# GpSimd's elementwise work outside the gated-MLP stage moved to the vector engine, in a two-layer fp32 trunk

## The chip, the cores and the metric

One of the eight cores of a Trainium2 chip runs the whole program; the other cores are idle. The metric is the device time of one execution in microseconds (us), taken as the median of several executions. The engines of the core are TensorE (PE, matrix products), VectorE (DVE, elementwise work and reductions), ScalarE (ACT, activations and copies), GpSimd (POOL, elementwise work here) and SyncE (SP, which issues most of the DMAs). Each has its own queue of instructions and takes them in order; semaphores tie the queues together.

## The reference

Two layers of a diffusion trunk, in float32. 512 latent tokens and 256 context tokens of width 1024 go through the same weights; the second (last) layer has outputs for the latent tokens alone.

```python
h = modulate(rms_norm(x, mix_pre_g[l]), sh1, sc1)
p = h @ w_in[l]                                   # 1024 x 8704
q = apply_rope(q_heads(p, q_norm_g[l]), cos, sin) # 8 heads of 128
k, v = kv_heads(p[..., K_OFF:GU_OFF], k_norm_g[l])# 2 key/value heads
attn = latent_attention(q, k_all, v_all)          # softmax over context + latent keys
# three branches, merged by sigmoid gates:
a_out = attn @ w_attn_o
g_out = chunk_spatial_gate(gelu(gu), rms_norm(gelu(gv)), ws, bs) @ w_gmlp_o
c_out = conformer_conv(...)                       # 31 taps, layer norm, silu, @ w_conv_o
y = (ga * a_out + gg * g_out + gc * c_out) @ w_out
x = x + g1 * rms_norm(y, mix_post_g[l])
h2 = modulate(rms_norm(x, ffn_pre_g[l]), sh2, sc2)
x = x + g2 * rms_norm(jnp.square(jax.nn.relu(h2 @ w_ff1)) @ w_ff2, ffn_post_g[l])
```

## The kernel before

Every large product is made of three products of rounded parts. `wload` fetches a 512 KB weight tile into `raw` (two buffers, `wraw`, and in some stages a few more, `xraw`), ScalarE rounds it to `hi` (`whi`, L171), and a second engine writes the rest `lo = raw - hi` (`wlo`, L174); there are four buffers each of `whi` and `wlo`. Which engine makes `wlo` is an argument, `pool_lo`: True is GpSimd, False the vector engine. Activations are split the same way by `split` (L178 on ScalarE, L179 on the vector engine). TensorE then runs hi*hi, hi*lo and lo*hi (`gemm_t` L192, `gemm_n` L206, `streamed` L494).

A layer has these stages, one behind the other, each with its own pool of SBUF buffers:

- attention. Keys and values, then four pairs of query heads. One softmax step is 128 queries of one head: scores (L635), row maximum (L639, vector), the negative maximum times the scale (`nb`, L642, vector), the exponential on ScalarE (L645), the reciprocal of its sum (L647, vector), the scaling of `Pm` by it (L648, GpSimd), transposes (L658), the split of the transposed tile (L661 ScalarE, L662 vector) and the product with the values (L669). Transposes come two steps behind the scores. In between TensorE works on fill: the projections of the next pair of heads (`q_stage`), the attention output (`attn_o`) and the sigmoid gates (`gate_a`). `rope` (L565 to L568) rotates queries and keys; its third product (L567) is on GpSimd.
- the gated-MLP stage with the 31-tap convolution on the vector engine (`gmlp_conv`), then the rest of the convolution branch (`conv_out`).
- `w_out` by `natural`, in units of 256 columns. The last unit of a token group is followed by `post_norm` (L440 to L452, the residual) and `pre_norm` (L398, transposes, L424 to L428), whose result the feed-forward part reads.
- the feed-forward part in four chunks `ch`: `up` makes relu (L1174, ScalarE), its square (L1175, GpSimd) and the split; `streamed` or `natural` brings it down to `Y`, which in the last chunk is multiplied by the gain (L1216, GpSimd) before the last norms.

The order of each engine's queue is not the order of the code: a scheduler that walks a simulated timeline lays the instructions out, with its own idea of how long each takes. So an operation that changes its engine also changes its place among its new neighbours, and can move neighbours on other engines.

Of the kernel before, what the change touches and what calls it, by code (L numbers as in the profile page):

```python
# [54 lines left out]
def trunk_kernel(ctx: ExitStack, tc: tile.TileContext, x, c, ctx_in, c_ctx, ada_w, ada_b, mix_pre_g, mix_post_g,  # L55
# [152 lines left out]
    def wload_n(src, pool_lo=False):  # L208
        return [wload(src[0:512], 4, 256, pool_lo), wload(src[512:1024], 4, 256, pool_lo)]
# [291 lines left out]
    def attention(l, hT, T, last, md, w_kv=None):  # L501
# [58 lines left out]
        def rope(o, C, S):  # L560

            ov = o[:, 0:4, :].rearrange("p i (h d) -> p i h d", h=2)
            for h in range(2):
                t2 = t_([P, 4, HD], "rt2", 1)
                nc.vector.tensor_tensor(t2[:, :, 0:64], ov[:, :, h, 64:], S[:, :, 0:64], ALU.mult)  # L565
                nc.vector.tensor_tensor(t2[:, :, 64:], ov[:, :, h, 0:64], S[:, :, 64:], ALU.mult)
                nc.gpsimd.tensor_tensor(ov[:, :, h, :], ov[:, :, h, :], C, ALU.mult)  # L567
                nc.vector.tensor_tensor(ov[:, :, h, :], ov[:, :, h, :], t2, ALU.add)  # L568

        def to_heads(o, h, g, ntok, tag, bufs):  # L570
# [12 lines left out]
            return hi, lo  # L583

        def q_stage(p, q):
            ws = wload_n(W[:, Q0 + 256 * p:Q0 + 256 * p + 256], True)
            o = t_([P, NT, 256], "pn", 1)
            for i0 in range(0, NT, 2):
                ps = ps1()
                for i in range(2):  # L590
                    gemm_n(ps[:, i * 256:(i + 1) * 256], (i0 + i) * P, ws, hT)
                    yield 2.6
                nc.scalar.copy(o[:, i0:i0 + 2, :], ps.rearrange("p (i c) -> p i c", c=256))
            rq = head_rstd(o, NT)
            sc = t_([P, 12], "sc", 2)
            nc.vector.tensor_scalar(sc[:, :2 * NT], rq[:, :2 * NT], SCALE, None, op0=ALU.mult)
            nsc = t_([P, 12], "nsc", 2)
            nc.vector.tensor_scalar(nsc[:, :2 * NT], rq[:, :2 * NT], -SCALE, None, op0=ALU.mult)
            rope(o, Cq, Sq)
            q[p] = (o, sc, nsc, p // 2)  # L600
# [11 lines left out]
        for i in range(6):  # L612
            for h in range(2):
                t = k_nat[:, i, h * HD:(h + 1) * HD]
                nc.gpsimd.tensor_scalar(t, t, rs[:, 2 * i + h:2 * i + h + 1], 1.0, op0=ALU.mult, op1=ALU.mult)
        rope(k_nat, Ck, Sk)
        q = {}
        for _ in q_stage(0, q):
# [6 lines left out]
        def S_step(qT, qs, h, i):  # L625
# [19 lines left out]
            nc.scalar.activation(Pm[:, :nk], ps[:, :nk], AF.Exp, bias=nb, scale=sc[:, col:col + 1], accum_out=sm)  # L645
            rc = t_([P, 1], "rc", 4)
            nc.vector.reciprocal(rc, sm)  # L647
            nc.gpsimd.tensor_scalar(Pm[:, :nk], Pm[:, :nk], rc, 1.0, op0=ALU.mult, op1=ALU.mult)  # L648
            return Pm

        def T_step(Pm, PT, attn, kv, i):
# [23 lines left out]

        def attn_o(p, attn):
            for u in range(2):
                w = wload(w_attn_o[l, p * 256:(p + 1) * 256, u * 512:(u + 1) * 512], 2, 512, True)
                for cc in range(4):
                    cidx = u * 4 + cc  # L680
                    if p == 0:
# [15 lines left out]
                        gated(cidx)  # L697

        def gated(cidx):
            nc.gpsimd.tensor_tensor(acc[cidx], acc[cidx], sga[cidx], ALU.mult)  # L700
            nc.scalar.dma_start(md[cidx], acc[cidx])

        def gate_tile(p, cidx):
# [18 lines left out]

        def gate_a(p, cidx):
            off = GATE0 + cidx * P
            w = wload(W[:, off:off + P], KB, P, True)
            sg = gate_tile(p, cidx)
            for s0, n in parts:
                ps = ps1()
                gemm_t(ps, w, hT, T, parts=[(s0, n, 0)])
                nc.scalar.activation(sg[:, s0:s0 + n], ps[:, :n], AF.Copy if p < 4 else AF.Sigmoid)  # L730
                yield 24 * n / 2400
            if p == 0:
                spilled[cidx] = dram.tile([P, T], F32, name=nm("sgd"))
                nc.sync.dma_start(spilled[cidx], sg)
            else:
                sga[cidx] = sg
# [308 lines left out]
    with stage("start", 6):  # L1045
# [36 lines left out]
                next(small, None)  # L1082
        for _ in small:
            pass
        w_kv = wload_kv(0, True, (0, 1))
        ada = [ada_shift_scale(j) for j in range(4)]
        next(ada[0])
        x_columns(LAT)
        w_kv += wload_kv(0, True, (2, 3))
        x_columns(CTXG)  # L1090
        for j in range(4):
            if j < 3:
# [7 lines left out]
    for l in range(DEPTH):  # L1100
# [25 lines left out]
        with stage("ffn", 4 if last else 2):  # L1126
# [35 lines left out]
            with here(ACT_E):  # L1162
                root = o_([P, 12], "rsq", 2)
                nc.scalar.activation(root[:, 0:1], eps, AF.Sqrt)
            natural(w_out[l], mh, [[g] for g in groups], 1, sink, after, True)
            Y = [t_([P, D], "Y", NT) for _ in range(NT)]
            for ch in range(4):
                fs = [(o_([P, T], "hT", 16, F32R), o_([P, T], "hT", 16, F32R)) for _ in range(8)]

                def up(j, w, s0, n):  # L1170
                    ps = ps2()
                    gemm_t(ps, w, h2, T, parts=None if n == T else [(s0, n, 0)])
                    f = t_([P, T], "ff", 2)
                    nc.scalar.activation(f[:, :n], ps[:, :n], AF.Relu)  # L1174
                    nc.gpsimd.tensor_tensor(f[:, :n], f[:, :n], f[:, :n], ALU.mult)  # L1175
                    hi, lo = fs[j]
                    split(hi[:, s0:s0 + n], lo[:, s0:s0 + n], f[:, :n])

                def w_up(j):
                    col = ch * 1024 + j * P  # L1180
                    return wload(w_ff1[l, :, col:col + P], KB, P, ch == 0)

                rest = range(8)
                if ch == 0:
# [19 lines left out]
                def sink2(grp, u, ps):  # L1204
# [7 lines left out]
                    if ch == 3:  # L1212
                        s = slice(u * 256, (u + 1) * 256)
                        squares(grp, u, lambda i: Y[grp[0] + i][:, s])
                        for i in range(grp[1]):
                            nc.gpsimd.tensor_tensor(Y[grp[0] + i][:, s], Y[grp[0] + i][:, s], gb[grp[2]][:, s], ALU.mult)  # L1216

                def after2(g):
                    post_norm(X, Y, g, ssq[g], out if last else None, last and g[0] == 2)
# [42 lines left out]
```

## Time and profile before

| what | value |
|---|---|
| three executions | 2683.68, 2689.81, 2682.62 us; median 2683.68 |
| the profiled execution | 2690.7 us, of which the span of its instructions is 2688.9 |
| mean granted TensorE clock | 0.989 of full speed |
| TensorE busy | 2608.4 us (97% of the span) |
| vector engine busy | 1552.3 us (58%) |
| ScalarE busy | 1076.1 us (40%) |
| GpSimd busy | 914.7 us (34%) |
| HBM | 111 GB/s over the span |

"Busy" is the sum of the time in which an engine had an instruction in work. A busy TensorE is a matter of records whose ends are modelled, so 97% says that it hardly waited, not that it was at its peak. The granted clock is the share of full speed that TensorE was given, here either 1 (2.4 GHz) or one half (1.2 GHz) in a stretch. Every time below is of the profiled execution.

### The profile page before, as it was taken

Reading aid. Unit: us, or ns where it says so; the run is one execution under the profiler, and the core shown is the slowest. Engines: PE = TensorE matmul, PEld = TensorE weight load, DVE = VectorE, ACT = ScalarE, POOL = GpSimd, SP = SyncE. Lnnn points to the kernel's source line nnn. Section 1 sums busy time; section 2 is a strip of 40 time slices with the busy share of each in tenths; the row PEclk is TensorE's granted clock in tenths of the full one; section 3 lists DMA queues with packets and bytes.
Section 4 is the critical chain, followed back from the end, with each engine's and each line's share of the span. In section 5 each row is a group of like instructions: output and inputs, shape, how many; then the busy total and the mean of one; then the engine's idle time right before and its main releaser. Section 6 shows DMA issues by size and latency. Waiting matters only on the chain.

```text
span 2688.9 us, 37915 instructions
## 1 busy us (share of the span) xinstructions
PE 2608.4 (97%) x15133; PEld 2277.3 (85%) x15133; DVE 1552.3 (58%) x2325; ACT 1076.1 (40%) x1848; POOL 914.7 (34%) x648
## 2 busy tenths in 40 slices
PE   6999999999999998999999999999999999999998
PEld 4989988888888898888888899888888888988888
DVE  4635735578864548445564367665479845633335
ACT  3546533443234635422121255555243234533324
POOL 2423336465463203402010133434555510421113
PEclk8999999999999999999999999999999999999999
DMA  6210134232345344243454342212433455433333
GB/s 233 61 56 32 32 98 138 73 93 85 105 135 173 105 160 141 79 127 112 138 188 133 118 157 72 65 32 67 126 102 102 141 155 176 137 118 100 97 95 110
DMA packets 322241, 300.13 MB, mean 112 GB/s; under 512 B 11517, under 2 KB 268817, under 8 KB 322065
## 3 DMA queue, kind: packets, MB, share of 16 engines
q1 hardware_dynamic: 309360, 271.20, 32.6%
q10 hardware_dynamic: 12704, 26.51, 2.8%
q8 instruction: 119, 1.95, 0.3%
q14 instruction: 58, 0.47, 0.1%
HBM read 275.63 MB, written 22.04 MB: 111 GB/s over the span
## 4 chain that ended last, share of the span: by engine, by line
PE 84%; DVE 9%; ACT 3%; DMA 3%; issue 1%; POOL 1%; SPq 0%; ACTq 0%; DVEq 0%; POOLq 0%
PE ps L192 44%; PE ps L494 16%; PE pq L192 7%; PE ps L206 6%; PE pq L206 3%; PE pq L669 3%; PE ps L635 2%; PE ps L658 1%; DVE wlo L174 1%; ACT whi L171 1%; PE ps L919 1%; DVE hB L428 1%; PE ps L532 1%; DMA xraw<-in_ada_w_dram 1%; DMA wraw<-in_w_in_dram 0%
## 5 line engine op out<-in xcount | busy, mean ns | idle before, releaser
L192 PE MATMUL ps<-hB,whi 128*128 128x512 f32 (+1 forms) x2272 | 595.3, 360 | 3.9 <-ACT hB L427 1.6
L174 POOL TENSOR_TENSOR wlo<-wraw,whi 128x1024 fp32r<-128x1024 f32 x160 | 388.3, 2430 | 519.4 <-ACT whi L171 507.2
L171 ACT CAST whi<-wraw 128x1024 fp32r<-128x1024 f32 x261 | 274.3, 1051 | 649.0 <-PE ps L192 325.3
L192 PEld LDWEIGHTS ps<-hB,whi 128*128 128x128 f32 x2272 | 389.7, 189 | 71.3 <-ACT ff L1174 2.3
L837 DVE SCALAR_TENSOR_TENSOR cy<-G,cw,cy 128x768 f32<-128x768 f32 (+1 forms) x464 | 404.3, 887 | 11.5
L192 PE MATMUL ps<-hB,wlo 128*128 128x512 f32 (+1 forms) x1136 | 373.2, 359 | 0.0
L494 PE MATMUL ps<-whi,hT 128*128 128x512 f32 x1152 | 357.1, 390 | 0.0
L1175 POOL TENSOR_TENSOR ff<-ff 128x512 f32<-128x512 f32 (+2 forms) x76 | 111.9, 1473 | 627.1 <-ACT ff L1174 626.9
L192 PE MATMUL ps<-hT,whi 128*128 128x512 f32 (+1 forms) x1408 | 319.1, 344 | 0.6 <-ACT gu L915 0.6
L494 PEld LDWEIGHTS ps<-whi,hT 128*128 128x128 f32 x1152 | 216.3, 188 | 45.7 <-issue 0.8
L192 PEld LDWEIGHTS ps<-hT,whi 128*128 128x128 f32 x1408 | 221.3, 189 | 34.4 <-ACT gu L915 1.1
L206 PE MATMUL ps<-whi,hT 128*128 128x256 f32 x1280 | 235.5, 286 | 0.7 <-ACT whi L171 0.7
L192 PEld LDWEIGHTS ps<-hB,wlo 128*128 128x128 f32 x1136 | 200.5, 189 | 32.0 <-DVE wlo L174 0.2
L494 PE MATMUL ps<-wlo,hT 128*128 128x512 f32 x576 | 224.1, 389 | 0.0
L174 DVE TENSOR_TENSOR wlo<-wraw,whi 128x1024 fp32r<-128x1024 f32 x101 | 133.8, 1326 | 154.6 <-ACT whi L171 151.2
L171 ACT CAST whi<-xraw 128x1024 fp32r<-128x1024 f32 x109 | 114.3, 1049 | 246.7 <-PE ps L494 116.9
L174 DVE TENSOR_TENSOR wlo<-xraw,whi 128x1024 fp32r<-128x1024 f32 x91 | 113.1, 1244 | 166.0 <-ACT whi L171 165.7
L206 PEld LDWEIGHTS ps<-whi,hT 128*128 128x128 f32 x1280 | 202.1, 194 | 1.4 <-ACT whi L171 0.9
L192 PE MATMUL ps<-hT,wlo 128*128 128x512 f32 x704 | 190.4, 344 | 0.0
L206 PE MATMUL ps<-wlo,hT 128*128 128x256 f32 x640 | 182.2, 285 | 1.3 <-DVE wlo L174 1.3
L343 POOL TENSOR_TENSOR asum<-asum,aprod 128x512 f32<-128x512 f32 x84 | 111.3, 1325 | 108.6 <-ACT aprod L341 66.1
L648 POOL TENSOR_SCALAR Pm<-Pm,rc 128x768 f32<-128x768 f32 (+1 forms) x80 | 68.4, 856 | 215.0 <-DVE rc L647 157.4
(300 smaller groups left out, 4654.2 us busy)
## 6 DMA issues: line engine op xcount, KB each, us to landing
wraw<-in_w_in_dram SPq DMA_DIRECT2D x134, 512.0 KB, 3.7
xraw<-in_w_ff_dram SPq DMA_DIRECT2D x89, 512.0 KB, 4.0
wraw<-in_w_ff_dram SPq DMA_DIRECT2D x63, 512.0 KB, 3.9
xraw<-in_ada_w_dram SPq DMA_DIRECT2D x39, 512.0 KB, 4.7
wraw<-in_ada_w_dram SPq DMA_DIRECT2D x33, 512.0 KB, 3.8
araw<-in_ada_w_dram SPq DMA_DIRECT2D x48, 256.0 KB, 2.9
xraw<-in_w_out_dram SPq DMA_DIRECT2D x18, 512.0 KB, 8.4
wraw<-in_w_attn_o_dram SPq DMA_DIRECT2D x16, 512.0 KB, 3.9
```

The source lines that it names most:

```text
L171: nc.scalar.copy(hi, raw)
L174: e.tensor_tensor(lo, raw, hi.bitcast(F32), ALU.subtract)
L192: nc.tensor.matmul(ps[:, d0:d0 + n], wt[:, k, c0:c0 + P], xt[:, s0:s0 + n], start=k == 0 and j == 0, stop=k == nk - 1 and j == 2)
L206: nc.tensor.matmul(o, xt[:, tok0:tok0 + P], wt, start=k == 0 and j == 0, stop=k == nk - 1 and j == 2)
L343: nc.gpsimd.tensor_tensor(sums[r], sums[r], t, ALU.add)
L428: nc.vector.tensor_tensor(lo[:, s], t, hi[:, s].bitcast(F32), ALU.subtract)
L494: nc.tensor.matmul(o, xt[:, tok], wt[:, k, :], start=kt == k == j == 0, stop=kt == 3 and k == 1 and j == 2)
L635: nc.tensor.matmul(ps[:, s0 - key0:s0 - key0 + n], a[:, i * P:(i + 1) * P], b[:, s0:s0 + n], start=m == 0, stop=m == 2)
L648: nc.gpsimd.tensor_scalar(Pm[:, :nk], Pm[:, :nk], rc, 1.0, op0=ALU.mult, op1=ALU.mult)
L669: nc.tensor.matmul(po[:, :256], a[:, kt0 + kt, vs], b[:, kt, :], start=kt == 0 and m == 0, stop=kt == nkt - 1 and m == 2)
L837: nc.vector.scalar_tensor_tensor(done if t == TAPS - 1 else y, G[:, :, t:t + 256], cw[:, t * 8 + cidx:t * 8 + cidx + 1], y, op0=ALU.mult, ...
L1175: nc.gpsimd.tensor_tensor(f[:, :n], f[:, :n], f[:, :n], ALU.mult)
```

## The change

Outside `gmlp_conv` each elementwise instruction of GpSimd becomes one of the vector engine, with the same operands. Two differ in form: the square of the feed-forward part now multiplies the product in PSUM with the relu, and the scalings have one scalar in place of two. What stays on GpSimd are the gated-MLP stage, the sums `asum` (L343) of the modulation vectors beside it, and two adds at the very end (L450). Clearing of tiles stays there too.

```diff
@@ rope
-                nc.gpsimd.tensor_tensor(ov[:, :, h, :], ov[:, :, h, :], C, ALU.mult)
+                nc.vector.tensor_tensor(ov[:, :, h, :], ov[:, :, h, :], C, ALU.mult)
@@ q_stage
-            ws = wload_n(W[:, Q0 + 256 * p:Q0 + 256 * p + 256], True)
+            ws = wload_n(W[:, Q0 + 256 * p:Q0 + 256 * p + 256])
@@ attention, keys
-                nc.gpsimd.tensor_scalar(t, t, rs[:, 2 * i + h:2 * i + h + 1], 1.0, op0=ALU.mult, op1=ALU.mult)
+                nc.vector.tensor_scalar(t, t, rs[:, 2 * i + h:2 * i + h + 1], None, op0=ALU.mult)
@@ S_step
-            nc.gpsimd.tensor_scalar(Pm[:, :nk], Pm[:, :nk], rc, 1.0, op0=ALU.mult, op1=ALU.mult)
+            nc.vector.tensor_scalar(Pm[:, :nk], Pm[:, :nk], rc, None, op0=ALU.mult)
@@ attn_o
-                w = wload(w_attn_o[l, p * 256:(p + 1) * 256, u * 512:(u + 1) * 512], 2, 512, True)
+                w = wload(w_attn_o[l, p * 256:(p + 1) * 256, u * 512:(u + 1) * 512], 2, 512)
@@ gated
-            nc.gpsimd.tensor_tensor(acc[cidx], acc[cidx], sga[cidx], ALU.mult)
+            nc.vector.tensor_tensor(acc[cidx], acc[cidx], sga[cidx], ALU.mult)
@@ gate_a
-            w = wload(W[:, off:off + P], KB, P, True)
+            w = wload(W[:, off:off + P], KB, P)
@@ the start
-        w_kv = wload_kv(0, True, (0, 1))
+        w_kv = wload_kv(0, False, (0, 1))
-        w_kv += wload_kv(0, True, (2, 3))
+        w_kv += wload_kv(0, False, (2, 3))
@@ w_out and feed-forward
-            natural(w_out[l], mh, [[g] for g in groups], 1, sink, after, True)
+            natural(w_out[l], mh, [[g] for g in groups], 1, sink, after)
-                    nc.gpsimd.tensor_tensor(f[:, :n], f[:, :n], f[:, :n], ALU.mult)
+                    nc.vector.tensor_tensor(f[:, :n], ps[:, :n], f[:, :n], ALU.mult)
-                    return wload(w_ff1[l, :, col:col + P], KB, P, ch == 0)
+                    return wload(w_ff1[l, :, col:col + P], KB, P)
-                            nc.gpsimd.tensor_tensor(Y[grp[0] + i][:, s], Y[grp[0] + i][:, s], gb[grp[2]][:, s], ALU.mult)
+                            nc.vector.tensor_tensor(Y[grp[0] + i][:, s], Y[grp[0] + i][:, s], gb[grp[2]][:, s], ALU.mult)
```

Three places show what the scheduler makes of it on the vector engine. The first is layer 0 behind `w_out`, where the residual of the first 256 tokens (`X_9233`, `X_9234`) is followed by their second norm (`rsv_9673` to `rs_9672`, then L398). Before:

```order
L452 SCALAR_TENSOR_TENSOR X_9233<-Y_9239,rs_9656,X_9233 128x1024
L452 SCALAR_TENSOR_TENSOR X_9234<-Y_9240,rs_9656,X_9234 128x1024
L1154 TENSOR_TENSOR Y_9241<-ps_9749,Gb_9262 128x256
L1154 TENSOR_TENSOR Y_9242<-ps_9749,Gb_9262 128x256
L142 TENSOR_SCALAR rsv_9673<-ss_9669 128x2
L146 RECIPROCAL rst_9677<-rsq_9675 128x2
```

The same place now:

```order
L452 SCALAR_TENSOR_TENSOR X_9233<-Y_9239,rs_9656,X_9233 128x1024
L452 SCALAR_TENSOR_TENSOR X_9234<-Y_9240,rs_9656,X_9234 128x1024
L174 TENSOR_TENSOR wlo_9875<-wraw_9871,whi_9873 128x1024
L1154 TENSOR_TENSOR Y_9241<-ps_9749,Gb_9262 128x256
L1154 TENSOR_TENSOR Y_9242<-ps_9749,Gb_9262 128x256
L174 TENSOR_TENSOR wlo_9881<-wraw_9877,whi_9879 128x1024
L142 TENSOR_SCALAR rsv_9673<-ss_9669 128x2
L146 RECIPROCAL rst_9677<-rsq_9675 128x2
```

Two weight splits that stood in GpSimd's queue (`wlo_9875`, `wlo_9881`) have come between the residual and the norm; five more follow before the second norm of the next 256 tokens.

The second place is a softmax step of layer 1 (row maximum `mx_16164`, its product `nb_16166`), with two products of `rope` for the next heads in between. Before:

```order
L639 TENSOR_REDUCE mx_16164<-ps_16157 128x1
L565 TENSOR_TENSOR rt_2590_16274<-pn_16001,S_14844 128x4x64
L566 TENSOR_TENSOR rt_2590_16274<-pn_16001,S_14844 128x4x64
L642 TENSOR_TENSOR nb_16166<-mx_16164,nsc_15671 128x1
L647 RECIPROCAL rc_16171<-sm_16169 128x1
```

The same place now:

```order
L174 TENSOR_TENSOR wlo_16561<-wraw_16557,whi_16559 128x1024
L639 TENSOR_REDUCE mx_16164<-ps_16157 128x1
L565 TENSOR_TENSOR rt_2590_16274<-pn_16001,S_14844 128x4x64
L566 TENSOR_TENSOR rt_2590_16274<-pn_16001,S_14844 128x4x64
L174 TENSOR_TENSOR wlo_16567<-wraw_16563,whi_16565 128x1024
L642 TENSOR_TENSOR nb_16166<-mx_16164,nsc_15671 128x1
```

One split stands ahead of the row maximum, one between it and `nb`.

The third place is a softmax step of context queries in layer 0 (`mx_1887`, `nb_1889`). Before:

```order
L639 TENSOR_REDUCE mx_1887<-ps_1883 128x1
L642 TENSOR_TENSOR nb_1889<-mx_1887,nsc_1005 128x1
L662 TENSOR_TENSOR PT_1860<-ps_1861,PT_1859 128x6x128
L578 TENSOR_TENSOR qT_1878<-ps_1870,qT_1877 128x512
L647 RECIPROCAL rc_1894<-sm_1892 128x1
```

The same place now:

```order
L174 TENSOR_TENSOR wlo_2463<-wraw_2459,whi_2461 128x1024
L639 TENSOR_REDUCE mx_1887<-ps_1883 128x1
L662 TENSOR_TENSOR PT_1860<-ps_1861,PT_1859 128x6x128
L578 TENSOR_TENSOR qT_1878<-ps_1870,qT_1877 128x512
L642 TENSOR_TENSOR nb_1889<-mx_1887,nsc_1005 128x1
```

A split is ahead of the row maximum, and `nb` has fallen behind two other splits. SP's queue, which issues the weight loads, differs only by neighbours that changed places.

## Rows read from the trace of the kernel before

**Rows 1.** The page's part 1: busy time, share of the span, instructions.

```profile
PE 2608.4 (97%) x15133; PEld 2277.3 (85%) x15133; DVE 1552.3 (58%) x2325; ACT 1076.1 (40%) x1848; POOL 914.7 (34%) x648
```

**Rows 2.** Busy time of each engine by stretch; columns as its first line says.

```profile
core 0: us, PE busy (x) PEld busy (x) DVE busy (x) ACT busy (x) POOL busy (x), PEclk, DMA share, GB/s
0.00:37.40 37.40, 14.67 (x95) 9.69 (x95) 20.68 (x47) 17.89 (x30) 10.62 (x16) 0.88 0.89 305
...
100.00:402.00 302.00, 290.94 (x1992) 267.42 (x1991) 166.44 (x364) 147.21 (x330) 108.56 (x83) 0.99 0.17 56
402.00:1005.00 603.00, 595.91 (x3424) 518.37 (x3424) 385.65 (x428) 235.29 (x313) 280.41 (x202) 0.99 0.38 119
1005.00:1072.00 67.00, 60.19 (x435) 57.09 (x435) 55.03 (x93) 40.01 (x91) 27.84 (x10) 0.92 0.48 143
...
1605.00:1690.00 85.00, 79.84 (x626) 77.67 (x625) 64.42 (x146) 47.02 (x121) 31.22 (x29) 0.96 0.29 89
1690.00:1876.00 186.00, 176.74 (x1143) 157.26 (x1142) 114.74 (x225) 101.77 (x201) 75.62 (x54) 0.99 0.16 51
...
2275.00:2345.00 70.00, 63.12 (x488) 61.32 (x487) 46.74 (x75) 39.74 (x90) 27.89 (x15) 0.95 0.59 190
...
2677.70:2688.90 11.20, 2.82 (x24) 2.62 (x22) 5.29 (x16) 2.84 (x8) 3.91 (x4) 0.79 0.24 94
```

**Rows 3.** GpSimd's groups by line: count, busy us, mean ns, idle before.

```profile
L174 POOL TENSOR_TENSOR wlo<-wraw,whi 128x1024 fp32r<-128x1024 f32 x160 | 388.3, 2430 | 519.4 <-ACT whi L171 507.2 <-PE ps L919 11.8
L1175 POOL TENSOR_TENSOR ff<-ff 128x512 f32<-128x512 f32 (+2 forms) x76 | 111.9, 1473 | 627.1 <-ACT ff L1174 626.9
L648 POOL TENSOR_SCALAR Pm<-Pm,rc 128x768 f32<-128x768 f32 (+1 forms) x80 | 68.4, 856 | 215.0 <-DVE rc L647 157.4 <-PE pq L192 16.2 <-DVE nb L642 14.5
L1216 POOL TENSOR_TENSOR Y<-Y,Gb 128x256 f32<-128x256 f32 x40 | 39.1, 995 | 72.6 <-ACT junk L1145 72.6
```

**Rows 4.** The vector engine's groups, shapes kept apart.

```profile
L174 DVE TENSOR_TENSOR wlo<-wraw,whi 128x1024 fp32r<-128x1024 f32 x101 | 133.8, 1326 | 154.6 <-ACT whi L171 151.2 <-PE ps L970 3.0
...
L690 DVE TENSOR_TENSOR acc<-acc,pq 128x512 f32<-128x512 f32 x48 | 32.8, 684 | 27.8 <-PE pq L192 27.8
...
L1154 DVE TENSOR_TENSOR Y<-ps,Gb 128x256 f32<-128x256 f32 x40 | 15.0, 417 | 10.9 <-ACT junk L1145 10.7
...
L398 DVE TENSOR_SCALAR xn<-X,rs 128x1024 f32<-128x1024 f32 x6 | 4.1, 748 | 0.0
```

**Rows 5.** Timelines of DVE and of POOL around 178 us: start, us, instruction.

```profile
172.35 0.16 DVE L642 TENSOR_TENSOR nb<-mx,nsc 128x1 f32<-128x1 f32 x1
...
178.93 1.80 DVE L642 TENSOR_TENSOR nb<-mx,nsc 128x1 f32<-128x1 f32 x1
...
178.37 2.34 POOL L174 TENSOR_TENSOR wlo<-wraw,whi 128x1024 fp32r<-128x1024 f32 x1 [4.25 <-ACT whi L171]
```

**Rows 6.** From 1000 to 1085 us: the chain's shares by line; DVE's and POOL's timelines.

```profile
by line: PE ps L192 26.1%; PE ps L206 16.2%; DVE X L452 10.9%; DVE hB L428 10.2%; DVE wlo L174 8.7%; PE pq L403 4.3%; DVE rsv L142 4.1%; ACT whi L171 3.5%; DVE Y L1154 3.2%; issue 2.9%; DVE Y L398 2.0%; DVE hf L424 1.9%; ACT junk L1145 1.6%
...
1043.77 5.19 DVE L428 TENSOR_TENSOR hB<-hf,hB 128x256 fp32r<-128x256 f32 x2
...
1039.69 6.43 POOL L174 TENSOR_TENSOR wlo<-xraw,whi 128x1024 fp32r<-128x1024 f32 x2 [12.30 <-ACT whi L171]
```

**Rows 7.** DVE's timeline behind `w_out` of layer 1.

```profile
2302.54 2.48 DVE L452 SCALAR_TENSOR_TENSOR X<-Y,rs,X 128x1024 f32<-128x1024 f32 x2
...
2309.93 2.38 DVE L148 TENSOR_TENSOR rst<-rst 128x2 f32<-128x2 f32 x1
2312.34 2.29 DVE L149 SCALAR_TENSOR_TENSOR rst<-rst,rsv 128x2 f32<-128x2 f32 x1
```

**Rows 8.** DVE's timeline in attention of layer 1.

```profile
1742.60 2.59 DVE L566 TENSOR_TENSOR rt<-pn,S 128x256 f32<-128x256 f32 x1
```

**Rows 9.** DVE's timeline at the start.

```profile
17.09 2.22 DVE L135 SCALAR_TENSOR_TENSOR rst<-rst,rsv 128x2 f32<-128x2 f32 x1
```

**Rows 10.** Busy time in one stretch of attention, columns as in rows 2.

```profile
268.00:335.00 67.00, 66.11 (x460) 60.92 (x458) 51.28 (x113) 34.58 (x75) 23.20 (x21) 1.00 0.10 32
```

## The prediction

> **What bounds the kernel now.** I read the page's busy times first: TensorE is busy 97% of the span, the vector engine 58%, GpSimd 34% [rows 1]. So the change can give back only time in which TensorE waits, or in which its clock is halved after a wait. The view by stretch says where that is [rows 2]: stretch less PE's busy time is 22.7 us at the start (37.4 - 14.7), 11.1 in layer 0's attention (100 to 402), 7.1 in 402 to 1005, 6.8 between `w_out` and the feed-forward part of layer 0 (1005 to 1072), 5.2 between the layers (1605 to 1690), 9.3 in layer 1's attention (1690 to 1876), 6.9 behind `w_out` of layer 1 (2275 to 2345) and 8.4 at the end. The five stretches in which GpSimd's moved work lies hold 39 us of waits (11.1 + 6.8 + 5.2 + 9.3 + 6.9). Their clock is 0.99, 0.92, 0.96, 0.99 and 0.95; one less that, times the stretch, is 3 + 5.4 + 3.4 + 1.9 + 3.5 = 17 us. Elsewhere TensorE runs without a pause, and no edit can win there.
>
> Then the timelines of these stretches, for what TensorE waits on. The reader is to see a small product `nb` on one column that takes 0.16 us, and the same one some us later that takes 1.80: it starts at 178.93 and ends at 180.73, where a weight split on GpSimd, begun at 178.37, ends as well (180.71) [rows 5]. So a vector instruction that begins beside a GpSimd instruction can stand still until that one is done. I looked at each longer wait of TensorE, and behind most of them the chain runs through such a stalled vector instruction: two of the feed-forward's input splits that take 5.19 us together beside 6.43 us of GpSimd splits [rows 6], two steps of a norm at 2.38 and 2.29 [rows 7], a rope product at 2.59 [rows 8], a step of a reciprocal root at 2.22 [rows 9].
>
> **The change: load.** It removes from GpSimd 82 weight splits (by the code: 4 at the start, 48 in attention, 10 in `w_out`, 20 in the first feed-forward chunk) at 2.43 us, 76 squares, 80 scalings and 40 gain products [rows 3], and 60 smaller ones (20 of `rope`, 16 gates, 24 of the keys; I put them at 1 us each): 199 + 112 + 68 + 39 + 60, some 480 us. On the vector engine two-operand work costs 0.417 us for 256 columns and 0.684 for 512 [rows 4], which is 0.267 for each further 256: 0.95 for 768 and 1.22 for 1024. (The group mean of its splits, 1.33, holds stalls.) So the splits cost 82 x 1.22 = 100 us. The squares are 32 of 512, 26 of 768 and 18 of 256 columns: 22 + 25 + 8 = 54. The gain products are 40 x 0.42 = 17. A scaling of 768 columns with one scalar is not in the trace; one of 1024 takes 0.75 [rows 4], which bounds it above, and a two-operand 256 (0.42) below. I take 0.6 for 64 of them and 0.4 for 16: 45 us, between 34 and 60. By the Trainium skill (VectorE: DVE Perf Modes, § The perf-mode tier table) an fp32 scaling over 2048 columns takes 1227 ns and a two-operand product 2293, and no run shows these sizes; that ratio on 0.95 would make the 64 scalings about 33 us. The 60 others at 0.3 to 0.8 are some 34. In all 250 us more on the vector engine, 1552 to about 1800, less the stalls that go. All of it is off the end as long as TensorE has other work: in 1072 to 1605 and 2345 to 2678, where the squares and gain products lie, TensorE does not wait on either engine, so these cost and give nothing. The squares hold their PSUM tile one vector instruction longer; there are three such tiles, and the next two products of TensorE cover that. Without this cover it would be 0.4 to 0.95 us for each of 76.
>
> **The change: stalls, by stretch.** 1005 to 1072: here the vector engine is the chain. It is busy 55 of 67 us. In the chain of 85 us its residual has 10.9% = 9.3 us for four instructions, which free of stalls are 2 x 2.48 [rows 7], so 4.3 stalled; the two `hB` splits take 5.19 for 0.8, 4.4 stalled; the norm's first step has 4.1% = 3.5 for some 0.5, 3.0 stalled [rows 6]. That is 11.7 us. In their place come seven weight splits, two of them right behind the residual as the order shows: 7 x 1.22 = 8.5. Gain 3 in waits, bounded by the 6.8 there and by 0 (if a split waits for its `whi`); with less of a wait I put 2 of the 5.4 us of halved clock on top: 5.
>
> 2275 to 2345: two steps stalled 2.2 and 2.1 [rows 7], each before a wait; one split comes between them and the next norm. Gain 4 (0 to 8).
>
> 1605 to 1690: splits and gain products replace stalls of about equal length between the layers; in the rope of the keys the chain gets much shorter (GpSimd's 24 small scalings and two products go), but TensorE waits there only 1 us at the end. Gain 1.5 (0 to 5).
>
> Attention of layer 1: the stalled rope product costs 2.2 us [rows 8], and the order puts one split of 1.22 there, with another ahead of the row maximum. Two such waits and the 1.9 us of clock: gain 4 (-10 to 11). Attention of layer 0: where 1.6 us of stall on `nb` go [rows 5], the order now has a split ahead of the row maximum and two others between it and `nb` (1.2 + 0.95 + 0.68), so that wait grows. Against it stand the first softmax steps and the scaling, shorter by 0.3 us. Gain 2.5 (-11 to 11).
>
> The start: two stalls like that of 17.09 [rows 9] become two splits of 1.22. But the DMA engines are 89% busy there [rows 2], so that an earlier start can be lost to them: 1 (0 to 4). The end: the last gain product is shorter and no longer stalls the norm: 1 (0 to 2). Against all this, splits queue on the vector engine for a `whi` or a free buffer, with the row maximum and transposed splits of the softmax behind them, for which TensorE waits: I take 2 us (0 to 10).
>
> The sum: 5 + 4 + 1.5 + 4 + 2.5 + 1 + 1 - 2 = 17 us. On the profiled execution, 2690.7, that is 2673.7. It lies 7 us above the median of the three runs, 2683.68, and what makes it so is not known; the difference is taken off the median: **2667 us**. What a measurement can tell from no change is about 0.3%, 8 us.
>
> **The rivals.** *Stalls turn into queueing (no change).* The third place of the order is the rule and not the exception: in attention each stall of 1.6 to 2.2 us is replaced by splits and other work ahead of `nb`, and only 1005 to 1072 and 2275 to 2345 gain, half of their 9: 2684 - 5 = 2679. For it: the scheduler fills every gap in front of a dependent instruction with a split. Against it: a split costs half on this engine.
>
> *The vector engine becomes the bound of attention (slower).* In 268 to 335 it is busy 51.3 of 67 us and GpSimd 23.2 [rows 10]; moved at 250/480, that is 12 more, 63 of 67. If work so interleaved can fill no more than that 51.3 of 67 (77%), this stretch grows by 63.3/0.77 - 67 = 15 us. Both attentions together have 281 us of vector work and 184 of GpSimd's in 488 [rows 2]: 281 + 96 is 77% of 488 on the mean, so about half of their seven such stretches lie above. Three and a half with half of that growth are 27 us, less 5 of stalls in the 281. It decides where vector work passes 77% of a stretch, and the time would be 2684 - 13 (the gains elsewhere) + 22 = 2693. Against it: the transposes come two steps behind the scores, which leaves each step room, and the 281 us hold more stalls than those 5. The Trainium skill (Perfetto Trace Analysis, § Optimizing Scalar/DVE Operations) says that with a saturated vector engine offloading to ScalarE or even GpSimd may make sense, though the two share an SBUF port; that speaks against this change, and by that rule the stretch at 268 would lose. At 58% over the span the trace does not bear it out.
>
> *The waits go nearly whole.* Most of the 39 us and half of the clock's 17 come back: 2684 - 38 = 2646.
>
> That the change is not made is no rival: GpSimd keeps 96 of its splits, all in the gated-MLP stage.
>
> **How the numbers follow.** Likeliest, 2667 (own range 2655 to 2676): 0.57. Waits nearly whole: 0.10. Turned into queueing: 0.19. Bound in attention: 0.14. The range 2648 to 2692 leaves out about half of the first and last rival, some 1 in 8; inside lie the bounds of the stretches taken a few at a time. Faster by over 0.3% (below 2676): 0.66, within: 0.20, slower: 0.14.
>
> **What would show it.** GpSimd's busy time near 435 us and the vector engine's between 1650 and 1750 (1552 + 250, less the stalls). Outside the gated-MLP stage no one-column vector instruction above 0.3 us. PE's wait in 1005 to 1072 down from 6.8 to about 3.5 with a higher clock, in 2275 to 2345 from 6.9 to about 3. In attention, waits on the row maximum and the transposed split (L639, L662) in place of those behind stalls; if they sum to more than 20 us over both layers, the bound in attention has it. I would be wrong if the vector engine's queue stands at a split that waits for `whi` while softmax work behind it is due.

## The result and the profile after

The changed kernel takes 2650.4 us (median of 4 runs, 2647.3 to 2652.2) beside 2684.8 for the kernel before in the same comparison: ratio 0.986, 95% interval 0.9848 to 0.9872, 34.4 us less. The forecast was 2667, which is 17 us less: the direction held, and the gain came out twice as large. The time lies inside the wide range of the forecast (2648 to 2692) and below the range of its likeliest case (2655 to 2676).

The profiled execution of the changed kernel took 2647.3 us, 3.1 below its median; that of before lay 5.9 above its own. So the two traces differ by 43.4 us, 9 more than the medians. Stretches below are compared by traces, whole edits by medians.

The page's first part after the change (before: [rows 1]):

```profile
PE 2591.1 (98%) x15133; PEld 2266.0 (86%) x15133; DVE 1658.5 (63%) x2663; ACT 1076.2 (41%) x1848; POOL 435.0 (16%) x310
```

GpSimd lost 480 us, as counted. The vector engine took over 250 us of work by the prediction's count and its busy time grew by 106: by that count the other 144 us are time in which it had stood still before and was counted as busy. (d_splits below measures this for the splits alone.) PE's 15133 products are the same and took 17.3 us less (2608.4 to 2591.1), at a mean granted clock of 0.996 in place of 0.989: that is the clock.

Busy time by stretch after the change, between the same products of TensorE as in [rows 2] (the row from 1048.20 is 1072 to 1605 of before, whose row stands in the second fence):

```profile
core 0: us, PE busy (x) PEld busy (x) DVE busy (x) ACT busy (x) POOL busy (x), PEclk, DMA share, GB/s
0.00:28.70 28.70, 12.79 (x95) 8.94 (x95) 15.58 (x45) 17.21 (x26) 1.28 (x12) 1.00 0.92 318
90.30:387.96 297.66, 289.82 (x1986) 266.36 (x1985) 195.78 (x441) 146.32 (x328) 2.74 (x1) 0.99 0.18 56
387.96:990.40 602.44, 595.37 (x3424) 518.01 (x3424) 391.28 (x431) 234.32 (x313) 276.53 (x199) 0.99 0.39 119
990.40:1048.20 57.80, 55.85 (x435) 53.91 (x435) 49.98 (x102) 40.29 (x91) 0.00 (x0) 1.00 0.55 166
1048.20:1578.20 530.00, 528.13 (x2967) 454.03 (x2966) 280.35 (x352) 152.98 (x227) 0.00 (x0) 1.00 0.41 129
1578.20:1661.00 82.80, 79.23 (x634) 78.11 (x633) 64.48 (x181) 49.00 (x123) 0.00 (x0) 0.96 0.30 91
1661.00:1838.30 177.30, 174.21 (x1142) 156.28 (x1141) 134.70 (x279) 102.97 (x203) 0.00 (x0) 1.00 0.17 54
2238.30:2300.60 62.30, 59.36 (x488) 58.27 (x487) 46.81 (x90) 39.35 (x90) 0.00 (x0) 1.00 0.66 212
2634.35:2645.50 11.15, 2.82 (x24) 2.62 (x22) 5.37 (x18) 2.83 (x8) 2.67 (x2) 0.83 0.24 94
```

```profile
1072.00:1605.00 533.00, 529.91 (x2976) 456.09 (x2975) 262.29 (x294) 154.59 (x231) 92.36 (x62) 1.00 0.41 129
```

Length less PE's busy time is again TensorE's wait. Against [rows 2]:

| stretch before | length | wait | PE busy | gain | forecast |
|---|---|---|---|---|---|
| start, to the first product of the keys | 37.4 to 28.7 | 22.7 to 15.9 | 14.7 to 12.8 | 8.7 | 1 |
| attention, layer 0 | 302.0 to 297.7 | 11.1 to 7.8 | 290.9 to 289.8 | 4.3 | 2.5 |
| 1005 to 1072, behind `w_out` | 67.0 to 57.8 | 6.8 to 1.9 | 60.2 to 55.9 | 9.2 | 5 |
| 1072 to 1605 | 533.0 to 530.0 | 3.1 to 1.9 | 529.9 to 528.1 | 3.0 | 0 |
| 1605 to 1690 | 85.0 to 82.8 | 5.2 to 3.6 | 79.8 to 79.2 | 2.2 | 1.5 |
| attention, layer 1 | 186.0 to 177.3 | 9.3 to 3.1 | 176.7 to 174.2 | 8.7 | 4 |
| 2275 to 2345, behind `w_out` | 70.0 to 62.3 | 6.9 to 2.9 | 63.1 to 59.4 | 7.7 | 4 |
| end | 11.2 to 11.15 | 8.4 to 8.3 | same | 0 | 1 |

That is 43.8 us; the four stretches left out of the table lie within 1.1 us each of before and are together 0.5 longer. The scheduler has changed the order of some products, so that the counts of a stretch differ by up to 9. Cut at equal counts, 1072 to 1605 gains 2.0 and 1605 to 1690 gains 3.2; the others stay within 0.7. Most stretches gave about twice their term, the start far more.

The vector engine's groups, shapes kept apart (before: [rows 4, 5]):

```profile
L174 DVE TENSOR_TENSOR wlo<-wraw,whi 128x1024 fp32r<-128x1024 f32 x165 | 204.7, 1241 | 201.1 <-ACT whi L171 196.8 <-PE ps L970 3.0
L648 DVE TENSOR_SCALAR Pm<-Pm,rc 128x768 f32<-128x768 f32 x64 | 39.6, 619 | 1.1
L642 DVE TENSOR_TENSOR nb<-mx,nsc 128x1 f32<-128x1 f32 x80 | 12.4, 155 | 0.6
```

The prices were right: a split takes 1.24 us (1.22 estimated), a scaling 0.62 (0.6). The small product `nb`, which had taken up to 2.09 before, has a mean of 0.155 over all 80 and takes 0.166 at most.

The vector engine's timeline behind `w_out` of layer 0 (before: [rows 6]), then TensorE's waits there, the two longest of before and the longest of after:

```profile
1025.45 2.48 DVE L452 SCALAR_TENSOR_TENSOR X<-Y,rs,X 128x1024 f32<-128x1024 f32 x2
1027.84 0.75 DVE L428 TENSOR_TENSOR hB<-hf,hB 128x256 fp32r<-128x256 f32 x2
...
1030.64 0.17 DVE L142 TENSOR_SCALAR rsv<-ss 128x2 f32<-128x2 f32 x1
1030.71 1.22 DVE L174 TENSOR_TENSOR wlo<-wraw,whi 128x1024 fp32r<-128x1024 f32 x1
...
1032.57 1.22 DVE L174 TENSOR_TENSOR wlo<-wraw,whi 128x1024 fp32r<-128x1024 f32 x1
```

```profile
1055.86 0.61 PE L403 MATMUL pq<-ident,Y 128*128 128x128 f32 x2 [4.79 <-DVE Y L398]
1059.98 1.65 PE L192 MATMUL ps<-hB,whi 128*128 128x512 f32 x3 [1.59 <-ACT hB L427]
```

```profile
1038.97 0.96 PE L192 MATMUL ps<-hB,whi 128*128 128x512 f32 x3 [1.95 <-ACT hB L427]
```

The two `hB` splits that took 5.19 beside GpSimd take 0.75. Two weight splits now stand inside the norm's chain, as the order had shown, and cost it 2.4 us; what was gained ahead of it and in it is more, for TensorE's waits in the stretch fell from 6.8 to 1.9 us.

### The profile page after: what moved, and what is told of

It reads as the page before. It is cut to its first block, busy times and chain, and to the rows that moved or that the text cites. A ratio compares the mean times of both kernels' runs of the same rounds, so it can differ in the third digit from the quotient of the medians.

```text
span 2645.5 us, 37736 instructions
## 1 busy us (share of the span) xinstructions
PE 2591.1 (98%) x15133; PEld 2266.0 (86%) x15133; DVE 1658.5 (63%) x2663; ACT 1076.2 (41%) x1848; POOL 435.0 (16%) x310
## 4 chain that ended last, share of the span: by engine, by line
PE 92%; DVE 3%; DMA 2%; ACT 2%; issue 1%; SPq 0%; DVEq 0%; ACTq 0%
PE ps L192 44%; PE ps L494 16%; PE ps L206 9%; PE pq L192 8%; PE pq L206 4%; PE pq L669 3%; PE ps L635 2%; PE ps L658 1%; PE ps L532 1%; DVE wlo L174 1%; ACT whi L171 1%; PE ps L919 1%; PE pq L403 0%; PE ps L574 0%; DMA xraw<-in_ada_w_dram 0%
## 5 line engine op out<-in xcount | busy, mean ns | idle before, releaser
L174 POOL TENSOR_TENSOR wlo<-wraw,whi 128x1024 fp32r<-128x1024 f32 x96 | 230.7, 2404 | 1549.2 <-ACT whi L171 1533.5
L174 DVE TENSOR_TENSOR wlo<-wraw,whi 128x1024 fp32r<-128x1024 f32 x165 | 204.7, 1241 | 201.1 <-ACT whi L171 196.8
L174 DVE TENSOR_TENSOR wlo<-xraw,whi 128x1024 fp32r<-128x1024 f32 x109 | 133.3, 1223 | 185.0 <-ACT whi L171 184.5
L343 POOL TENSOR_TENSOR asum<-asum,aprod 128x512 f32<-128x512 f32 x84 | 111.6, 1329 | 105.7 <-ACT aprod L341 63.2
L494 PEld LDWEIGHTS ps<-wlo,hT 128*128 128x128 f32 x576 | 108.1, 188 | 22.6 <-issue 0.4
L192 PEld LDWEIGHTS ps<-hT,wlo 128*128 128x128 f32 x704 | 110.2, 189 | 16.0
```

The source lines that it names most:

```text
L174: e.tensor_tensor(lo, raw, hi.bitcast(F32), ALU.subtract)
L192: nc.tensor.matmul(ps[:, d0:d0 + n], wt[:, k, c0:c0 + P], xt[:, s0:s0 + n], start=k == 0 and j == 0, stop=k == nk - 1 and j == 2)
L343: nc.gpsimd.tensor_tensor(sums[r], sums[r], t, ALU.add)
L494: nc.tensor.matmul(o, xt[:, tok], wt[:, k, :], start=kt == k == j == 0, stop=kt == 3 and k == 1 and j == 2)
```

## The experiments

Each kernel was timed in five rounds beside the kernel before:

| run | us | before | ratio | interval |
|---|---|---|---|---|
| a_start | 2677.8 | 2687.4 | 0.9961 | 0.9949 to 0.9974 |
| b_attn | 2673.8 | 2687.4 | 0.9947 | 0.9933 to 0.996 |
| c_out | 2674.4 | 2687.4 | 0.9948 | 0.9935 to 0.996 |
| d_splits | 2654.7 | 2686.6 | 0.9879 | 0.9866 to 0.9893 |
| e_products | 2681.1 | 2688.5 | 0.9974 | 0.9964 to 0.9983 |
| f2_shadow | 2717.4 | 2686.6 | 1.0114 | 1.01 to 1.0128 |
| g_shadow1 | 2671.5 | 2686.6 | 0.9941 | 0.9928 to 0.9953 |
| h_spin | 2683.9 | 2686.6 | 0.9987 | 0.9978 to 0.9996 |
| i_yield | 2640.3 | 2688.5 | 0.9822 | 0.9808 to 0.9835 |
| j_ff | 2646.7 | 2688.5 | 0.9847 | 0.9834 to 0.9861 |
| k_all | 2652.4 | 2688.5 | 0.9867 | 0.9854 to 0.9881 |
| l_both | 2638.9 | 2688.6 | 0.9816 | 0.9802 to 0.9829 |

The **theory**: the vector engine stands still beside GpSimd's instructions, TensorE waits for it, and pays again in clock. The main **rival**: TensorE waits for the moved work itself, which takes half the time on the vector engine.

**The change by place: a_start, b_attn, c_out.** Each is the kernel before with one third of the diff. The start alone:

```
-        w_kv = wload_kv(0, True, (0, 1))
+        w_kv = wload_kv(0, False, (0, 1))
...
-        w_kv += wload_kv(0, True, (2, 3))
+        w_kv += wload_kv(0, False, (2, 3))
```

> The kernel before with only the four splits of the start moved to the vector engine. Theory (stalls): the vector engine stood still beside GpSimd's splits, and TensorE, and with it the release of the raw tiles and the loads, stood behind it; then this edit alone gives about what the trace after shows there, 10 us: 2675, with the first product of the keys (L532) at about 28.5 us in place of 37.4. Rival (the loads are the bound, as the prediction had it): 0 to 4 us, 2681 to 2685.

Measured: 9.7 us from four splits, and the first product of the keys starts at 28.16. A start bound by its loads, as this run's rival had it, is out.

Attention alone: the lines of `rope`, `q_stage`, the keys, `S_step`, `attn_o`, `gated` and `gate_a`.

```
-            w = wload(W[:, off:off + P], KB, P, True)
+            w = wload(W[:, off:off + P], KB, P)
...
-            nc.gpsimd.tensor_scalar(Pm[:, :nk], Pm[:, :nk], rc, 1.0, op0=ALU.mult, op1=ALU.mult)
+            nc.vector.tensor_scalar(Pm[:, :nk], Pm[:, :nk], rc, None, op0=ALU.mult)
```

> The kernel before with only attention's work moved (splits, rope products, scalings of keys and of softmax, gates). Theory (stalls): the gain is made stretch by stretch, and the stretches add: 3.7 us of layer 0's attention and 8.6 of layer 1's, with little else, 12 us: 2672. Rival (the vector engine becomes the bound in attention): 0 or slower, 2684 to 2700.

Measured: 13.6 us. The vector engine did not become the bound in attention.

`w_out` and feed-forward alone: `natural`'s and `w_up`'s splits, the squares, the gain products.

```
-            natural(w_out[l], mh, [[g] for g in groups], 1, sink, after, True)
+            natural(w_out[l], mh, [[g] for g in groups], 1, sink, after)
...
-                    return wload(w_ff1[l, :, col:col + P], KB, P, ch == 0)
+                    return wload(w_ff1[l, :, col:col + P], KB, P)
```

> The kernel before with only the work of w_out and feed-forward moved (splits, squares, gain products). Theory (stalls, stretches add): 9.2 us behind w_out of layer 0, 2.9 in the feed-forward part, 2.3 between the layers, 7.7 behind w_out of layer 1, together 22: 2662. Rival (the stretches are not independent: what one gains is lost at the next): clearly less than 22.

Measured: 13.1 us, clearly less than 22, which is what the rival expected. The 22 was added up from the two traces, which are 9 us farther apart than the medians, and took in the part between the layers, which belongs to attention's diff: cut at equal counts of products, that stretch is 3.7 us shorter in b_attn's trace and not shorter in c_out's. The rival has a small part too: behind `w_out` of layer 1 this run gains 6.2 us of the 7.7, and attention of layer 1 is 1.7 longer. The three parts add: 9.7 + 13.6 + 13.1 = 36.4 against 34.4 for the whole.

**The change by kind: d_splits, e_products.** The first is the kernel before with only the 82 splits moved (every `True` or `ch == 0` of the diff changed and no other line), the second the reverse.

> The kernel before with only the 82 splits moved to the vector engine; squares, scalings, products of rope, gates and gains stay on GpSimd. They are 199 of the 480 us that the change takes from GpSimd, but its longest instructions (2.43 us beside 0.9 to 1.5). Theory (stalls): a vector instruction stands still for up to the rest of the instruction beside it, so the splits have most of it: 20 to 28 of the 34 us, 2656 to 2664. Rival (the gain goes by GpSimd's busy time): 199/480 of 34, 14 us, 2670.

> The kernel before with only the squares, the scalings and the products of rope, gates and gains moved, the 82 splits left on GpSimd: the other half of the change, 280 of its 480 us of GpSimd's time. If the parts add (34 less the 32 that the splits gave alone), 0 to 5 us are gained, 2682 to 2687; if they need each other (stalls that one alone leaves in the chain), 10 us or more here.

Measured: 31.9 us for the splits, more than expected, and 7.3 for the rest, between the two cases expected of it (31.9 + 7.3 is 39.2 of 34 to 36, so they share a little). The gain does not go by GpSimd's busy time: 41% of that brings nearly all. The vector engine's part of d_splits' first line says why:

```profile
PE 2594.1 (98%) x15133; PEld 2268.7 (86%) x15133; DVE 1556.6 (59%) x2407; ACT 1075.8 (41%) x1848; POOL 722.9 (27%) x566
```

It has 82 more instructions, 100 us at 1.22, and is busy only 4 us longer than in [rows 1]. So by this count some 96 us of its busy time before were standstill.

**GpSimd's instructions without the moved work: f2_shadow, g_shadow1.** The changed kernel, with an idle instruction in `wload` at the 82 places, whose result nobody reads (`pool_lo == 2` marks these places).

```
+        if pool_lo == 2:
+            idle = o_([P, nk, ncols], "adarows", 1, mybir.dt.float8e4)
+            nc.gpsimd.tensor_tensor(idle, hi.bitcast(F32), hi.bitcast(F32), ALU.subtract, saturate=False)
```

> The changed kernel, and beside each of the 82 splits that it moved GpSimd subtracts the same weight tile from itself into a scratch tile that nobody reads. No moved work goes back; the vector engine's work and the weights' are those of the changed kernel. Theory (stalls): GpSimd's reads alone hold up the vector engine, so that one-column products of 1.5 us and more are back outside the gated-MLP stage and 15 to 40 us of the gain go: 2665 to 2690. Rival (the gain is the shorter way of the moved work itself, 1.22 us in place of 2.43): the time stays at 2650, within 4 us.

Measured: 2717.4, 67 us above the changed kernel and beyond the upper end of what the theory gave. No moved work went back, so the rival cannot be the whole account; that it has a part is not excluded, and the start below bears on it. GpSimd's group, then the vector engine and GpSimd behind `w_out` of layer 0 (lines are 3 higher here: L455 is L452, L431 is L428, L1157 is L1154):

```profile
L177 POOL TENSOR_TENSOR adarows<-whi 128x1024 fp8e4<-128x1024 f32 x82 | 207.4, 2529 | 1316.2 <-ACT whi L171 1314.3
```

```profile
1041.69 5.75 DVE L455 SCALAR_TENSOR_TENSOR X<-Y,rs,X 128x1024 f32<-128x1024 f32 x2
...
1051.87 1.86 DVE L142 TENSOR_SCALAR rsv<-ss 128x2 f32<-128x2 f32 x1
...
1054.85 0.72 DVE L1157 TENSOR_TENSOR Y<-ps,Gb 128x256 f32<-128x256 f32 x2
...
1057.61 1.84 DVE L148 TENSOR_TENSOR rst<-rst 128x2 f32<-128x2 f32 x1
```

```profile
1040.66 5.71 POOL L177 TENSOR_TENSOR adarows<-whi 128x1024 fp8e4<-128x1024 f32 x2 [13.58 <-ACT whi L171]
1049.71 3.99 POOL L177 TENSOR_TENSOR adarows<-whi 128x1024 fp8e4<-128x1024 f32 x2 [3.34 <-ACT whi L171]
1054.25 5.19 POOL L177 TENSOR_TENSOR adarows<-whi 128x1024 fp8e4<-128x1024 f32 x2 [0.55 <-ACT whi L171]
```

The residual's two steps take 5.75 in place of 2.48, steps of the norm 1.86 and 1.84 in place of 0.16: the stalls of [rows 6, 7], made by instructions whose result nobody uses. They read a tile of 128x1024 and write one; whether the reading or the writing does it, the run does not tell. TensorE's longest waits for the vector engine are now these (after the change 1.3, 2.3 and 0.3 us):

```profile
PE pq L406 <- DVE Y L401: 10.2, 2, 6.4
PE ps L195 <- DVE ff L1178: 9.7, 4, 4.8
PE pq L672 <- DVE PT L665: 7.5, 4, 3.5
```

The idle instructions also hold the `whi` tiles longer, but ScalarE waits for that in only three places, 8.5 us in all. Over the span the vector engine's busy time is 1749.3, with the 2663 instructions that took 1658.5: 91 us of standstill. That is about what d_splits took away (96), yet it costs twice the time; it may be that the moved work, which is on the vector engine's queue here, leaves less slack to take it up.

The second run has a copy in place of the subtraction:

```
+            nc.gpsimd.tensor_copy(idle, hi.bitcast(F32))
```

> As the run before it, but GpSimd only copies the weight tile into the scratch tile: one input in place of two. If it is the two inputs of GpSimd's instruction that hold up the vector engine, the time stays at 2650 within 4 us and the one-column products at 0.16; if any elementwise instruction of GpSimd on SBUF does it, vector instructions stand still for up to the length of the copy and the time lies between 2655 and 2685, by the copy's length. Rival (the moved work's own way): 2650 in both.

```profile
L177 POOL CAST adarows<-whi 128x1024 uint8<-128x1024 f32 x82 | 135.6, 1654 | 1342.3 <-ACT whi L171 1341.5
```

Measured: 21 us above the changed kernel, and the vector engine busy 35 us longer (1693.9). An instruction with one input is enough to hold it up. The `nb` stayed at 0.16 at most, which was expected of the other case: none of the 80 began beside a copy.

**The clock by itself: h_spin.** The kernel before, and in `normed` of the second group behind `w_out` of layer 0, to which a tile `spin` is handed:

```
+        if spin is not None:
+            pt = ps1()
+            nc.tensor.matmul(pt[:, 0:n], ident, ss, start=True, stop=True)
+            with here(mybir.EngineType.PE):
+                for _ in range(18):
+                    nc.tensor.matmul(pt, spin[:, 0:P], spin[:, 0:512], start=True, stop=True)
```

> The kernel before, and in the wait of 4.8 us at 1050.8, once the squares of that norm are done, TensorE multiplies 18 times a tile that it has (128x512, some 4 us) into a PSUM tile that nobody reads. No wait on another engine gets shorter. Theory (the wait costs a second time, through the halved clock behind it): the 10.2 us at half clock at 1055.7 go or shrink and the stretch 1005 to 1072 is 3 to 5 us shorter, 2681. Rival (the clock is no cost of its own here): nothing or, where the extra products come late, up to 4 us lost.

```profile
1048.32 4.37 PE L401 MATMUL pq<-hT 128*128 128x512 f32 x18
1054.95 0.30 PE L409 MATMUL pq<-ident,Y 128*128 128x128 f32 x1 [1.42 <-DVE Y L404]
```

```profile
1006.20:1068.60 62.40, 60.51 (x456) 57.69 (x455) 51.84 (x86) 38.14 (x87) 28.00 (x10) 1.00 0.50 153
```

The columns of the second fence are those of [rows 2]. The stretch is 62.4 us beside 67.0 there, with the clock at 1.00 beside 0.92. Less the idle products, 4.5 us from 1048.2 to 1052.7, PE is busy 56.0 for the work that took 60.2 (55.9 after the change). TensorE's wait got hardly shorter: 1.9 us and the 4.5 of idle products stand in place of 6.8. So of the 9.2 us that this stretch gained by the change, 4.2 are clock. Over the whole run 2.8 us are measured (interval 1.1 to 5.9), at the edge of what can be told.

**The edges of it: k_all, j_ff, i_yield, l_both.** The changed kernel with GpSimd's last 96 splits moved too:

```
-        e = nc.gpsimd if pool_lo else nc.vector
+        e = nc.vector
```

> The changed kernel with the 96 splits of the gated-MLP stage on the vector engine as well. There TensorE waits 7 us in 590 in layer 0 and not at all in layer 1, and the vector engine is busy 389 of 590 and 276 of 385. 96 splits of 1.22 us are 117 more (about 75 and 42), 464 and 318, less stalls: below 80 per cent. Theory (only a stall on TensorE's chain costs): no change within 5 us, 2646 to 2655. Rival (with the splits the vector engine is late for TensorE here, as the prediction feared in attention): 2660 or more.

Measured: 2652.4, no change that can be told. The vector engine's busy time rose by 95 us (1658.5 to 1753.3) for 117 us of splits, so some 22 us of standstill ended and brought nothing: TensorE hardly waits there.

The square from SBUF:

```
-                    nc.vector.tensor_tensor(f[:, :n], ps[:, :n], f[:, :n], ALU.mult)
+                    nc.vector.tensor_tensor(f[:, :n], f[:, :n], f[:, :n], ALU.mult)
```

> The changed kernel with the square taken of the tile in SBUF (f times f) in place of PSUM times f, so that a PSUM tile is free one vector instruction sooner. TensorE waits for the square twice, 1.5 us at 2288 and 0.8 at 2309, and hardly anywhere else. If the held PSUM tile is that wait, 1 to 3 us are gained, 2648; the prediction put this hold at nothing, by which it is 2650.

Measured: 2646.7, but its interval overlaps the changed kernel's and the traces differ by 1 us. Not told apart from nothing.

The tails of the modulation vectors put off (`ada_finish` has become a generator):

```
-        ada_finish(l, v, nr, rows)
+        yield
+        yield from ada_finish(l, v, nr, rows)
...
+            yield
             n = nr * KB
             pg = ps1()
```

> The changed kernel, and the tail of each modulation vector (the transposes of its sums, and those of its gain) is put off by a step of its queue each, so that products stand in TensorE's order between a transpose and what it waits for. The changed kernel waits there 1.6 + 3.7 us at 618 to 624 (with 6.8 us at half clock behind them), 1.2 at 805 and 1.2 at 1374. Theory (a wait costs its length and, where the clock falls behind it, half of that stretch): up to 5.3 + 3.4 + 1 us, 2641 to 2646. Rival (the order only moves the wait elsewhere): 2650.

TensorE's waits between 600 and 660 us, first of the changed kernel, then of this one:

```profile
PE ps L381 <- DVE gg L378: 3.7, 1, 3.7
PE ps L363 <- ACT adarows L356: 1.6, 1, 1.6
```

```profile
PE ps L364 <- ACT adarows L356: 1.6, 1, 1.6
PE ps L192 <- ACT gu L917: 0.2, 1, 0.2
```

Measured: 2640.3, 10 us below the changed kernel (7.4 between the two traces). The wait of 3.7 us is gone, that of 1.6 stays. In this window PE's clock goes from 0.94 to 1.00, and TensorE fits 343 products into the 60 us in place of 317.

> The changed kernel with both of the edits that made it shorter: the tails of the modulation vectors put off by a step (10 us alone) and the squares taken of the tile in SBUF (3 to 4 us alone, hardly more than its measurement is uncertain). The waits lie in different stretches, so by the theory the gains add: 2636 to 2639. Rival (the 3 to 4 us of the squares are the difference between runs and not a gain, since the traces of the two show only 1 us): 2640.

Measured: 2638.9, 0.9816 (0.9802 to 0.9829), which overlaps i_yield: the squares add nothing that can be told. Both are faster than the changed kernel.

## Which step of the prediction failed, and what held

**The step that failed** is the size of two terms of the sum. The start stood there with 1 us, and its four splits gave 9.7 (a_start), half of the 17 us by which the sum fell short. The clock stood there with 2 of 5.4 us in one stretch and 1.9 in another, and by the traces it gave 17.3 over the span. The 39 us of waits in "the five stretches in which GpSimd's moved work lies" leave out the 22.7 of the start, though four of the moved splits lie there.

**Right.** The mechanism, the counts, the prices of the splits and scalings, the engines' busy times (435; 1650 to 1750), and that the cover of squares and gain products holds. f2_shadow shows the mechanism, which before was read from instructions that ended together. One-column instructions above 0.3 us outside the gated-MLP stage are gone but for one, a step of the last norm. It ends with one of the two adds that GpSimd kept:

```profile
2640.05 0.51 DVE L148 TENSOR_TENSOR rst<-rst 128x1 f32<-128x1 f32 x1
2637.88 2.67 POOL L450 TENSOR_TENSOR X<-X,Y 128x512 f32<-128x512 f32 x2 [496.32 <-ACT Y L449]
```

**Off: the start, "an earlier start can be lost to them: 1".** By a_start it is 9.7. The main waits of SP's queue in the first 40 us, before the change:

```profile
SPq L303 <- PE pq L310: 9.8, 4, 4.0
SPq L303 <- POOL wlo L174: 3.4, 3, 1.4
```

The DMA engines' busy share then, in tenths, one digit a microsecond:

```profile
DMA  0369999775899999999999999999999693697997
```

The first wait (the second is gone) and the DMA engines' share after the change:

```profile
SPq L303 <- PE pq L310: 3.5, 3, 2.0
```

```profile
DMA  0189999957899789999999999999999999999999
```

Before, the two stalled steps (2.2 us each, the first in [rows 9]) hold up the copy of `xT` behind them on the vector engine, and TensorE waits 3.3 us for its PSUM tile; the products of the modulation stand behind that, they hold the raw tiles, and SP's loads wait for the tiles. So the loads were late in good part because of the stall. A second part is the line of 3.4 us, in which the queue waits for GpSimd's splits themselves. In f2_shadow, where the splits stay on the vector engine and only stalls come back, the first product of the keys starts at 33.5: 4.8 of the 8.7 us are lost again. How much of the rest is the splits' own shorter time stays open. An 89% share says that the engines moved something, not that the first product waited for it: before, 37.4 us at 305 GB/s are 11.4 MB ahead of that product, after, 28.7 at 318 are 9.1.

**Off: the clock, "I put 2 of the 5.4 us of halved clock on top".** It was 4.2 there (h_spin) and 17.3 over the span, 40% of the traces' difference. The sum had 2 there, 1.9 in layer 1's attention and nothing elsewhere. Behind `w_out` of layer 1 the term for the wait, 4, was exact (6.9 to 2.9), and 3.8 of clock came on top.

**Off: attention, 2.5 + 4 "less 2 for splits queueing".** The two stretches got 4.3 and 8.7 us shorter, and b_attn, which also moves the keys' work between the layers, gained 13.6. The wait at the third place of the order, where [rows 5] have the stall, was to grow and fell from 3.2 to 2.5 us (the first line before, the second after, now behind the transposed split, as forecast), and TensorE's waits in both attentions fell from 20.3 to 10.9 us.

```profile
181.62 1.05 PE L658 MATMUL ps<-ident,Pm 128*128 128x128 f32 x6 [3.19 <-ACT Pm L645]
167.02 1.50 PE L658 MATMUL ps<-ident,Pm 128*128 128x128 f32 x6 [2.45 <-DVE PT L662]
```

The stretch of [rows 10] has the vector engine busy 58.1 of 67.7 us after the change, and TensorE waits 1.1:

```profile
253.20:320.90 67.70, 66.62 (x465) 61.31 (x464) 58.07 (x138) 35.62 (x78) 0.00 (x0) 1.00 0.10 32
```

So the 77% that the rival took for the most that can be filled was no limit: at 86% TensorE hardly waits. And part of what it counted as work was standstill, for it added up 63 us here and 58 are measured. By the Trainium skill (Perfetto Trace Analysis, § Optimizing Scalar/DVE Operations) handing work of a saturated vector engine to GpSimd may make sense, though between these two it might not help; with the vector engine at 86% here, taking work from GpSimd paid.

**Off, small.** 1072 to 1605 gave 2 to 3 us, not 0: a transpose of a modulation vector waited 3.1 us from 1398 and now waits 1.2. The end gave nothing.

By its number the third rival, the waits nearly whole, at 2646, came nearest; by its account it did not come true. Of the 39 us of waits in its five stretches 20 came back, and of their 17 us of clock 12. The start, which it did not count, gave 9 more, so that its number is in part luck. What stays open is how the standstill divides between shortening TensorE's waits directly and letting work behind it start earlier; the runs show only their sum.

## What to carry to other kernels

Before sharing elementwise work between GpSimd and the vector engine, compare one small vector instruction inside and outside GpSimd's spans. Where it differs, GpSimd's work can cost the vector engine a quarter to half of its length, as it did here (35 of 136 us, 91 of 207, 96 of 199), and the vector engine's busy share holds that standstill. Price a stalled chain by the gap on TensorE plus nearly half of each stretch at half clock behind it (4.2 us for some 10 here). A busy DMA share is no reason to write off a stall ahead of it: see first whether the queue that issues the loads waits for a tile.

## What the runs showed of the hardware

- An instruction of GpSimd with one input in SBUF was enough: 82 copies of 1.65 us put 35 us on the vector engine's time, 82 subtractions of 2.53 us put 91. Beside the subtractions a product of PSUM with SBUF ran at its usual length (0.72 for two, L1157 at 1054.85), while steps on two columns in SBUF took 1.84 to 1.86 in place of 0.16. That agrees with the Trainium skill (SBUF — State Buffer, § Who interferes with whom): a vector instruction with two inputs in SBUF contends with a GpSimd instruction that reads SBUF, one with at most one input there does not, outside the modes that take both ports. The norm's first step, with one input, stood still too (1.86 at 1051.87); whether it ran in such a mode no run shows.
- The steps of the convolution, the vector engine's largest group, did not stand still beside GpSimd: they read one input from SBUF and their accumulator `cy` from PSUM. After the change 152 of the 232 with 768 columns began inside a GpSimd instruction of over 0.6 us and took 1.021 us on the mean, 1.025 at most; the 59 that met none took 1.022. The gates that now run beside GpSimd's splits of the gated-MLP stage, with two inputs in SBUF, did: 2.98 us in place of 0.96.

```profile
L837 DVE SCALAR_TENSOR_TENSOR cy<-G,cw,cy 128x768 f32<-128x768 f32 x232 | 237.1, 1022 | 7.4
```

- In the kernel before, behind a wait of 4.8 us at 1050.8, TensorE's products ran at half clock for some 10 us (granted clock 0.51 from 1055.7 to 1066, 0.92 over the stretch); with products of no use in most of that wait they ran at full clock (1.00 over the stretch).
